# Seven-product gate and up in all four feed-forwards, with sums in place and SSM preparation moved to the down products

## The chip, the cores and the metric

The kernel runs on one core of one Trainium2 chip. The metric is the device time of one execution in microseconds (us). The engines are TensorE (PE, with its weight loads PEld), VectorE (DVE), ScalarE (ACT), GpSimd (POOL) and SyncE (SP), which issues most DMAs. Each engine works through its own instructions in order.

## The reference

One inference step of a trunk of two layers. Each layer adds half a feed-forward, a mixer, and half a second feed-forward to the residual x (1024 wide), all in fp32:

```python
def swiglu(h, w_gu, w_down):
    gate, up = jnp.split(h @ w_gu, 2, axis=-1)
    return (jax.nn.silu(gate) * up) @ w_down
...
every layer: x += 0.5*FFN_a(rms(x)); x += MIX(rms(x)); x += 0.5*FFN_b(rms(x))
```

In layer 0 the mixer is a depthwise convolution beside sliding-window attention, in layer 1 a grouped complex SSM with a GLU. There are 528 prompt positions (16 learned ones and 512 tokens) and 8 sample tokens, 536 columns in all. The hidden width of a feed-forward is 2816, which is 22 tiles of 128.

## The kernel before

x lies transposed in eight tiles x[0] to x[7] of 128 rows and 536 columns; a "half" is 268 of them. A product of fp32 precision is made of three matmuls of rounded parts: each operand is split into a part hi (written by ScalarE, L128, L226 or `put`'s L148) and the rest lo (subtracted on VectorE, L129, L227, L149), and TensorE adds hi·hi, hi·lo and lo·hi. Weights come by DMA into four buffers `raw`, and their parts go into three buffers `whi` and three `wlo`.

The four feed-forwards are called A, B (layer 0) and C, D (layer 1) here. `ffn` takes the 22 tiles in chunks of 8, 8 and 6: first gate and up of each tile of the chunk, which end in the subtraction that writes `ml`, then eight down products, each of which adds to one x tile (L428). After the last chunk `finalize` prepares the next stage's operands from x.

- In A and B a tile of gate and up is `gemm` twice: 96 matmuls of 268 columns. VectorE splits two weights (L129) and multiplies and adds (L406, L408, L409, L149).
- In C and D (`STRASSEN = (3, 5)`) `seven` makes a tile from seven products P1 to P7 of half the depth and half the columns, 84 matmuls (L268). It needs sums of weights (`seven_weights`, L230 to L235) and of operands (`operands`: xh, eh and fh with their lo parts), and additions afterwards (L272 to L290).

A tile framework orders the instructions of each engine from the code's priorities, its own time estimates and the buffers. Work that doesn't belong to a feed-forward is put between its steps by a generator, `filler`: `setup0` (tables for the first mixer) in A, and `ssm_prep` (tables for the SSM, mostly complex multiplications on VectorE at L877 to L883 and L1039 to L1046) in B, two steps after each gate and up tile but a chunk's last two, and two after each of six down products:

```python
                if filler is not None and i < nf - 2:
                    next(filler, None)
                    next(filler, None)
```

`load` brings in x, transposes it, and runs tile 0 of A's gate and up (`head`) product by product as each x tile arrives.

Of the kernel before, what the change touches and what calls it, by code (L numbers as in the profile page):

```python
# [18 lines left out]
D = 1024  # L19
# [13 lines left out]
STRASSEN, DMASUM = (3, 5), False  # L33
# [29 lines left out]
class Trunk:  # L63
# [87 lines left out]
    def finalize(self, d, g):  # L151

        nc = self.nc
        col = self.g[:, g * 8 + d:g * 8 + d + 1]
        x = self.x[d]
        if g in STRASSEN:
            self.operands(d, col)
# [17 lines left out]
    def extra(self, pool):  # L175

        self.fx = pool
# [29 lines left out]
    def seven_weights(self, gu, f):  # L207
# [1247 lines left out]
```

## Time and profile before

| | |
|---|---|
| Median of 3 runs | 2038.1 us (2034.99 to 2038.55) |
| Profiled execution | 2040.23 us |
| Its span in the trace | 2038.4 us |
| Busy: PE, DVE, ACT, POOL | 1978.1, 1378.6, 790.1, 113.5 us |
| Feed-forward A, from the load's end to the last x update | 48.7 to 428.7 us |
| First mixer | 428.7 to 662.9 us |
| Feed-forward B | 662.9 to 1068.0 us |
| Feed-forward C | 1068.0 to 1445.4 us |
| Second mixer and D | 1445.4 to 2038.4 us |

The span runs from the first to the last instruction that the profiler recorded; the execution's own time is 1.8 us longer. The stages are cut at the end of VectorE's update of x[7], since the next stage's first products need it soon after.

### The profile page before, as it was taken

The numbers are of one execution on the slowest core, as the hardware profiler recorded it, in microseconds if no ns is written. First come the engines' busy times: TensorE is split into PE (matmuls) and PEld (weight loads), VectorE is DVE, ScalarE is ACT, GpSimd is POOL, SyncE is SP. The second block draws the span as 40 slices with busy tenths as digits, with TensorE's granted clock in tenths as the row PEclk, the third lists the DMA queues.
The fourth block names the chain that finished last, engine by engine and source line by source line (L and its number), as shares of the span: only waits on it lengthen the run. The fifth ranks groups of instructions, "written<-read, shape, count | busy, mean of one in ns | idle before, by whom it ended". The sixth has DMA issues, their size and how long they took to land.

```text
span 2038.4 us, 37681 instructions
## 1 busy us (share of the span) xinstructions
PE 1978.1 (97%) x15774; PEld 1924.3 (94%) x15774; DVE 1378.6 (68%) x2263; ACT 790.1 (39%) x1274; POOL 113.5 (6%) x172
## 2 busy tenths in 40 slices
PE   6999999999989999999998999999999999999997
PEld 5999999998869999999998999999988999999997
DVE  4533433478977888666478859677795589587686
ACT  4322222333446332322255525345334455254353
POOL 2000000012200002112000000000110000000000
PEclk9999999999969999999999999999999999999998
DMA  6423333232005435446322323324783323233331
GB/s 177 123 87 90 89 88 94 73 85 59 27 6 122 124 127 161 127 122 172 103 83 78 109 83 94 104 83 148 191 260 109 89 73 111 87 94 94 94 92 55
DMA packets 371499, 213.52 MB, mean 105 GB/s; under 512 B 36119, under 2 KB 362323, under 8 KB 370921
## 3 DMA queue, kind: packets, MB, share of 16 engines
q1 hardware_dynamic: 354897, 190.63, 32.4%
q0 software_dynamic: 5872, 19.40, 3.3%
q8 instruction: 124, 2.03, 0.4%
q10 hardware_dynamic: 10560, 1.09, 0.4%
q14 instruction: 46, 0.38, 0.1%
HBM read 193.14 MB, written 23.65 MB: 106 GB/s over the span
## 4 chain that ended last, share of the span: by engine, by line
PE 89%; DVE 6%; ACT 2%; DMA 1%; issue 1%; SPq 1%; ACTq 0%; DVEq 0%
PE mm L139 28%; PE mm L268 19%; PE mm L142 14%; PE S L139 12%; PE S L142 6%; PE S L268 3%; DVE yc L566 1%; PE S L739 1%; DVE wlo L129 1%; DMA raw<-in_ffn_w_gu 1%; ACT whi L128 0%; PE ms L747 0%; PE ms L753 0%; DMA mC<-dC 0%; PE ms L1028 0%
## 5 line engine op out<-in xcount | busy, mean ns | idle before, releaser
L128 ACT ACTIVATE whi<-raw 128x1024 fp32r<-128x1024 f32 (+2 forms) x236 | 235.2, 1000 | 665.5 <-PE mm L139 314.5
L129 DVE TENSOR_TENSOR wlo<-raw,whi 128x1024 fp32r<-128x1024 f32 (+2 forms) x236 | 272.7, 1157 | 59.8 <-ACT whi L128 55.6
L139 PE MATMUL mm<-xh,whi 128*128 128x268 f32 x1280 | 268.5, 292 | 8.8 <-DVE us L1128 2.6
L139 PE MATMUL mm<-xl,whi 128*128 128x268 f32 x1280 | 266.7, 289 | 0.0
L142 PE MATMUL mm<-xh,wlo 128*128 128x268 f32 x1280 | 266.5, 289 | 0.0
L139 PE MATMUL mm<-mh,whi 128*128 128x268 f32 x1188 | 252.3, 290 | 2.5 <-DVE ta L286 1.2
L142 PE MATMUL mm<-mh,wlo 128*128 128x268 f32 x1188 | 249.9, 287 | 0.9 <-DVE wlo L129 0.8
L139 PE MATMUL mm<-ml,whi 128*128 128x268 f32 x1188 | 250.0, 287 | 0.0
L139 PEld LDWEIGHTS mm<-xh,whi 128*128 128x128 f32 x1280 | 201.8, 191 | 11.3 <-issue 3.6
L142 PEld LDWEIGHTS mm<-xh,wlo 128*128 128x128 f32 x1280 | 202.2, 190 | 2.0 <-issue 1.7
L139 PEld LDWEIGHTS mm<-xl,whi 128*128 128x128 f32 x1280 | 202.6, 191 | 1.1 <-issue 0.5
L139 PEld LDWEIGHTS mm<-mh,whi 128*128 128x128 f32 x1188 | 188.1, 189 | 4.9 <-ACT whi L128 1.8
L142 PEld LDWEIGHTS mm<-mh,wlo 128*128 128x128 f32 x1188 | 187.8, 188 | 2.0 <-DVE wlo L129 1.5
L139 PEld LDWEIGHTS mm<-ml,whi 128*128 128x128 f32 x1188 | 188.5, 189 | 0.2
L226 ACT ACTIVATE whi<-raw 128x1024 fp32r<-128x1024 f32 x88 | 93.4, 1061 | 104.1 <-issue 42.9
L139 PE MATMUL S<-mh,whi 128*128 128x268 f32 x604 | 128.4, 288 | 0.6 <-ACT whi L128 0.6
L139 PE MATMUL S<-ml,whi 128*128 128x268 f32 x604 | 127.3, 287 | 0.0
L142 PE MATMUL S<-mh,wlo 128*128 128x268 f32 x604 | 127.2, 286 | 0.0
L227 DVE TENSOR_TENSOR wlo<-raw,whi 128x1024 fp32r<-128x1024 f32 x88 | 107.4, 1221 | 15.8 <-ACT whi L226 14.9
L268 PE MATMUL mm<-xh,whi 128*128 128x268 f32 x352 | 103.2, 293 | 4.7 <-ACT sn L278 2.9
L268 PE MATMUL mm<-eh,whi 128*128 128x268 f32 x352 | 103.1, 293 | 0.9 <-issue 0.7
L268 PE MATMUL mm<-xl,whi 128*128 128x268 f32 x352 | 102.1, 290 | 0.0
(522 smaller groups left out, 4365.7 us busy)
## 6 DMA issues: line engine op xcount, KB each, us to landing
raw<-in_ffn_w_gu SPq DMA_DIRECT2D x174, 512.0 KB
raw<-in_ffn_w_down SPq DMA_DIRECT2D x64, 512.0 KB
raw<-in_ffn_w_down SPq DMA_DIRECT2D x32, 384.0 KB
raw<-in_ssm_w_glu SPq DMA_DIRECT2D x16, 512.0 KB
raw<-in_ab_w_in SPq DMA_DIRECT2D x10, 512.0 KB
dB<-B POOLq DMA_DIRECT2D x8, 512.0 KB, 3.8
dC<-CL POOLq DMA_DIRECT2D x32, 128.0 KB, 3.1
dT<-dK POOLq DMA_DIRECT2D x8, 512.0 KB, 5.0
```

What stands on the lines that cost most here:

```text
L128: nc.scalar.activation(hi[:, :K], raw[:, :K], AF.Copy)
L129: nc.vector.tensor_sub(lo[:, :K], raw[:, :K], hi[:, :K].bitcast(F32))
L139: nc.tensor.matmul(ps[:, h, :HT], hi[:, k, :], src[:, h * HT:(h + 1) * HT], start=(k == 0 and i == 0), stop=False)
L142: nc.tensor.matmul(ps[:, h, :HT], lo[:, k, :], xh[k][:, h * HT:(h + 1) * HT], start=False, stop=(k == K - 1))
L226: nc.scalar.activation(h[:], r[:], AF.Copy)
L227: nc.vector.tensor_sub(l[:], r[:], h[:].bitcast(F32))
L268: nc.tensor.matmul(ps, w[:, c + k, :], b[k], start=bool(first and k + i == 0), stop=bool(last and k == 3 and i == 2), skip_group_check=True)
L566: nc.vector.scalar_tensor_tensor(y, z, wcol(c, j), y, op0=OP.mult, op1=OP.add)
L739: nc.tensor.matmul(S[:, g, :w], qT[t][rw, 128 * b:128 * b + 128], kT[rw, k0:k0 + w], start=False, stop=True)
```

## The change

- `STRASSEN` holds all four feed-forwards, so A (but for tile 0, which stays in the load) and B use `seven` too.
- The chunks are 6, 8 and 8 tiles.
- The sums of weights are made in the `raw` buffers themselves; the buffer S goes.
- `operands` scales x anew (`scaled`) instead of keeping the scaled tiles of the first four.
- At the start of a feed-forward P1 and P5 of tiles 0 and 1 come first.
- The load makes `operands` too; for d below 4 it also splits the unsummed right half, into mh[4+d].
- `filler` runs over down products only: one step for each in a chunk of 6, two in a chunk of 8, one for four of the last chunk. `ssm_prep` therefore runs over B and C, and makes its table E in two halves.

```diff
-STRASSEN, DMASUM = (3, 5), False
+STRASSEN = (0, 2, 3, 5)
+CHUNKS = ((0, 6), (6, 8), (14, 8))
...
+    def scaled(self, d):
+        w = self.fx.tile([128, NT], F32, name="ou", bufs=2)
+        self.nc.scalar.activation(w[:], self.x[d][:], AF.Copy, scale=self.col(d))
+        return w
...
+        u = self.scaled(d)
         if d < 4:
...
-            self.put(self.xh[d][:], self.xl[d][:], w[:])
+            if plain:
+                self.put(plain[0][:, l], plain[1][:, l], u[:, r])
+            nc.vector.tensor_sub(u[:, r], u[:, l], u[:, r])
+            self.put(self.xh[d][:], self.xl[d][:], u[:])
             return
-        w, b = self.t1[k], self.b12[k]
-        u, e, f = t("ou"), t("oe"), self.fx.tile([128, HT], F32, name="of")
-        nc.scalar.activation(u[:], x[:], AF.Copy, scale=col)
         self.put(self.xh[d][:], self.xl[d][:], u[:])
-        nc.vector.scalar_tensor_tensor(e[:, l], w[:, r], -1.0, u[:, r], op0=OP.mult, op1=OP.subtract)
-        nc.vector.tensor_sub(e[:, r], u[:, r], b[:])
+        w = self.scaled(k)
+        e, f = self.fx.tile([128, NT], F32, name="sn", bufs=2), self.fx.tile([128, HT], F32, name="u3")
+        nc.vector.tensor_sub(e[:, r], u[:, r], w[:, r])
+        nc.vector.scalar_tensor_tensor(e[:, l], e[:, r], -1.0, w[:, l], op0=OP.mult, op1=OP.subtract)
         self.put(self.eh[k][:], self.el[k][:], e[:])
         nc.vector.scalar_tensor_tensor(f[:], e[:, l], -1.0, u[:, l], op0=OP.mult, op1=OP.subtract)
         self.put(self.fh[k][:], self.fl[k][:], f[:])
...
         split(gh, gl, G)
-        if not DMASUM:
-            nc.vector.tensor_add(S[:, k1], U[:, k0], U[:, k1])
-        nc.vector.tensor_add(S[:, k0], S[:, k1], G[:, k0])
-        split(sh, sl, S)
-        nc.vector.tensor_add(q[:], S[:, k0], G[:, k1])
-        if not DMASUM:
-            nc.vector.tensor_add(U[:, k0], U[:, k0], G[:, k0])
+        nc.vector.tensor_add(q[:], U[:, k0], U[:, k1])
+        split(qh, ql, q)
+        nc.vector.tensor_add(U[:, k0], U[:, k0], G[:, k0])
+        nc.vector.tensor_add(G[:, k0], G[:, k0], q[:])
+        nc.vector.tensor_add(G[:, k1], G[:, k1], G[:, k0])
+        split(sh, sl, G)
         split(uh, ul, U)
-        split(qh, ql, q)
...
+        early = {(0, "P1"): -4, (0, "P5"): -3, (1, "P1"): -2, (1, "P5"): -1} if f0 + n0 == 0 else {}
+        key = lambda a: early.get(a, 7 * a[0] + SLOTS[a[1]])
+        for n, p in sorted(((n, p) for n in range(nf - n0) for p in SLOTS), key=key):
...
             def products(k):
+                h, l = [self.xh[k][:, :HT], self.xh[k][:, HT:]], [self.xl[k][:, :HT], self.xl[k][:, HT:]]
+                if k < 4:
+                    h[1], l[1] = self.mh[4 + k][:, :HT], self.ml[4 + k][:, :HT]
                 for f in range(2):
-                    self.gemm(acc[f], (whi[f], wlo[f]), self.xh, self.xl, ks=(k,))
+                    for i, (w, b) in enumerate(((whi[f], h), (whi[f], l), (wlo[f], h))):
+                        for j in range(2):
+                            nc.tensor.matmul(acc[f][:, j, :HT], w[:, k, :], b[j], start=k + i == 0, stop=k + i == ND + 1)
...
-                nc.scalar.activation(self.xh[d][:], x, AF.Copy, scale=col)
-                nc.vector.scalar_tensor_tensor(self.xl[d][:], x, col, self.xh[d][:].bitcast(F32),
-                                               op0=OP.mult, op1=OP.subtract)
+                self.operands(d, (self.mh[4 + d], self.ml[4 + d]) if d < 4 else None)
...
-        for f0, nf in ((0, 8), (8, 8), (16, 6)):
-            if seven:
-                self.seven(gu, f0, nf)
-            for i in range(0 if seven else nf):
...
+        filler = iter(filler)
+        for f0, nf in CHUNKS:
+            last = f0 + nf == D_FF // 128
+            if f0 == 0 and head:
+                self.rstd()
...
-                self.put(self.mh[i][:], self.ml[i][:], b[:])
-                if filler is not None and i < nf - 2:
-                    next(filler, None)
-                    next(filler, None)
+                self.put(self.mh[0][:], self.ml[0][:], b[:])
+            self.seven(gu, f0, int(f0 == 0 and head is not None), nf)
...
-                if f0 == 16:
+                if last:
                     self.finalize(d, gnext)
-                if filler is not None and d < 6 and f0 < 16:
-                    next(filler, None)
-                    next(filler, None)
+                fill((1 if nf < 8 else 2) if not last else int(d < 4))
...
+        with self.tc.tile_pool(name="spe", bufs=1) as se:
+
+            for q0 in (0, 16):
+                qs = slice(q0, q0 + 16)
+                e = [se.tile([128, 16, NCK], F32, name=f"E{i}") for i in range(2)]
+                nc.vector.memset(e[0][:, :, 0], 1.0)
+                nc.vector.memset(e[1][:, :, 0], 0.0)
...
+                        if n > 4:
+                            yield
...
+                ZC = lambda: sj.tile([128, 1152], F32, name="Z")[:]
...
+                CL = ZC().rearrange("p (q r s c) -> p q r s c", q=4, r=2, s=9)
...
+        scope = self.extra()
+        self.project(2)
+        sp, fx = ExitStack(), []
         prep = self.ssm_prep(sp.enter_context(tc.tile_pool(name="sp", bufs=1)))
-
-        def then():
-            self.finish(prep)
-            sp.close()
-            self.extra(fx.enter_context(tc.tile_pool(name="fx", bufs=1)))
-
-        self.ffn(io["ffn2_w_gu"][0], io["ffn2_w_down"][0], 3, prep, then=then)
-        self.ffn(io["ffn1_w_gu"][1], io["ffn1_w_down"][1], 4, seven=fx)
-        fx = ExitStack()
-        self.mixer1(5, lambda: self.extra(fx.enter_context(tc.tile_pool(name="fx", bufs=1))))
-        self.ffn(io["ffn2_w_gu"][1], io["ffn2_w_down"][1], None, fin=True, seven=fx)
+        more = lambda: fx.append(self.extra())
+        self.ffn(io["ffn2_w_gu"][0], io["ffn2_w_down"][0], 3, scope, prep, then=more)
+        self.ffn(io["ffn1_w_gu"][1], io["ffn1_w_down"][1], 4, fx.pop(), prep)
+        self.finish(prep)
+        sp.close()
+        self.mixer1(5, more)
+        self.ffn(io["ffn2_w_gu"][1], io["ffn2_w_down"][1], None, fx.pop(), fin=True)
```

VectorE, among the down products of B's second chunk, before (x_80 is x[3], L1039 to L1046 and L878 to L883 are `ssm_prep`, w and Z its buffers):

```order
L428 SCALAR_TENSOR_TENSOR x_80<-S,x_80 128x536
L1041 TENSOR_TENSOR CL<-w_9945,w_9946 128x4x144
L129 TENSOR_TENSOR wlo<-raw,whi 128x1024
L1056 COPY BD<-bb 64x8x16 x2
L1065 TENSOR_TENSOR K<-ms,dd 128x16
L1043 TENSOR_TENSOR w_9945<-C,pw 128x576
L1044 TENSOR_TENSOR w_9946<-C,pw 128x576
L1045 TENSOR_TENSOR w_9945<-w_9945,w_9946 128x576
L1046 TENSOR_SCALAR CL<-w_9945 128x4x144
L878 TENSOR_TENSOR w_10265<-bb,pw 128x512
L877 TENSOR_TENSOR w_10264<-bb,pw 128x512
L428 SCALAR_TENSOR_TENSOR x_81<-mm,x_81 128x536
```

and after (`ssm_prep` at L877 and L1044 ff., x update L423, weights of the next gate and up at L222 to L229, down weights L130):

```order
L423 SCALAR_TENSOR_TENSOR x_80<-mm,x_80 128x536
L1044 TENSOR_TENSOR w_11246<-C,pw 128x576
L1045 TENSOR_TENSOR w_11247<-C,pw 128x576
L225 TENSOR_TENSOR q_10136<-raw 128x512
L130 TENSOR_TENSOR wlo<-raw,whi 128x1024
L227 TENSOR_TENSOR raw<-raw 128x512
L222 TENSOR_TENSOR ql<-q_10136,qh 128x512
L423 SCALAR_TENSOR_TENSOR x_81<-mm,x_81 128x536
L130 TENSOR_TENSOR wlo<-raw,whi 128x1024
L423 SCALAR_TENSOR_TENSOR x_82<-S,x_82 128x536
```

What moved: between these two x updates stood ten instructions of `ssm_prep` and one weight split; now two of `ssm_prep` stand between x[3] and x[4], with sums and splits of the next chunk's weights.

VectorE, among the gate and up tiles of B's second chunk, before (L406, L408, L409 and L149 are one tile's gate and up, L129 a weight split):

```order
L406 TENSOR_TENSOR ta<-S,R 128x536
L1046 TENSOR_SCALAR CL<-w_9317 128x4x144
L878 TENSOR_TENSOR w_9699<-bb,pw 128x512
L129 TENSOR_TENSOR wlo<-raw,whi 128x1024
L877 TENSOR_TENSOR w_9698<-bb,pw 128x512
L408 TENSOR_TENSOR tb<-mm,R 128x536
L409 TENSOR_TENSOR tb<-tb,ta 128x536
L879 TENSOR_TENSOR Z<-w_9698,w_9699 128x4x128
L129 TENSOR_TENSOR wlo<-raw,whi 128x1024
L881 TENSOR_TENSOR w_9698<-bb,pw 128x512
L882 TENSOR_TENSOR w_9699<-bb,pw 128x512
L149 TENSOR_TENSOR ml_114<-tb,mh_106 128x536
```

and after (L222 are splits, L225 and L227 to L229 sums of weights, L277, L283, L285 the additions and scalings of a tile):

```order
L222 TENSOR_TENSOR ql<-q_9303,qh 128x512
L228 TENSOR_TENSOR raw<-raw,q_9303 128x512
L277 TENSOR_TENSOR tb<-u_9195,mm 128x268
L285 TENSOR_TENSOR ta<-ta,R 128x536
L1050 TENSOR_TENSOR w_9804<-w_9804,w_9805 128x576
L229 TENSOR_TENSOR raw<-raw 128x512
L286 SCALAR_TENSOR_TENSOR tb<-tb,ta 128x536
L1051 TENSOR_SCALAR Z<-w_9804 128x4x144
L877 TENSOR_TENSOR w_9894<-bb,pw 128x512
L272 TENSOR_TENSOR ta<-sn,S 128x268
L876 TENSOR_TENSOR w_9893<-bb,pw 128x512
L222 TENSOR_TENSOR wlo<-raw,whi 128x1024
```

What moved: the tile's own rows come from `seven` and are more than twice as many, and rows of `ssm_prep`, issued at down products in the code, stand here still.

ScalarE at the start, before (L365 writes xh, L371 splits the head's weights, L374 makes squares, L362 copies x out of PSUM):

```order
L371 ACTIVATE whi<-raw 128x512
L362 ACTIVATE x_78<-S 128x536
L371 ACTIVATE whi<-raw 128x512
L365 ACTIVATE xh_86<-x_78,gcols 128x536
L374 ACTIVATE ta<-x_78 128x536
L365 ACTIVATE xh_85<-x_77,gcols 128x536
L374 ACTIVATE sq<-x_77 128x536
L362 ACTIVATE x_80<-S 128x536
L371 ACTIVATE whi<-raw 128x512
```

and after (L187 scales x into `ou`, L149 is `put`'s hi part, L373 and L376 what L371 and L374 were):

```order
L373 ACTIVATE whi<-raw 128x512
L366 ACTIVATE x_78<-S 128x536
L373 ACTIVATE whi<-raw 128x512
L376 ACTIVATE ta<-x_78 128x536
L187 ACTIVATE ou<-x_77,gcols 128x536
L376 ACTIVATE sq<-x_77 128x536
L187 ACTIVATE ou<-x_78,gcols 128x536
L366 ACTIVATE x_80<-S 128x536
L149 ACTIVATE mh_105<-ou 128x268
L149 ACTIVATE mh_106<-ou 128x268
L373 ACTIVATE whi<-raw 128x512
L376 ACTIVATE ta<-x_79 128x536
```

What moved: the two xh rows came right after the second weight split; now squares, scaled copies and hi parts of the right halves stand ahead of xh, which comes later than the rows shown.

## Rows read from the trace of the kernel before

**Rows 1.** The page: span, then busy time, share and instructions of each engine.
```profile
span 2038.4 us, 37681 instructions
...
PE 1978.1 (97%) x15774; PEld 1924.3 (94%) x15774; DVE 1378.6 (68%) x2263; ACT 790.1 (39%) x1274; POOL 113.5 (6%) x172
```

**Rows 2.** The page: shares of the chain that ended last, by engine.
```profile
PE 89%; DVE 6%; ACT 2%; DMA 1%; issue 1%; SPq 1%; ACTq 0%; DVEq 0%
```

**Rows 3.** Stretches: window, length, busy of PE, PEld, DVE, ACT, POOL, clock, DMA share, GB/s.
```profile
179.30:321.90 142.60, 142.60 (x1155) 142.60 (x1154) 56.69 (x65) 35.10 (x41) 0.00 (x0) 1.00 0.31 89
...
662.90:808.00 145.10, 145.10 (x1192) 143.76 (x1191) 126.15 (x323) 44.15 (x58) 14.33 (x27) 1.00 0.46 139
...
1068.00:1211.60 143.60, 136.76 (x1056) 134.02 (x1056) 108.59 (x162) 66.27 (x101) 0.00 (x0) 0.98 0.30 89
1211.60:1344.70 133.10, 132.42 (x1059) 131.10 (x1058) 97.74 (x137) 58.47 (x89) 0.00 (x0) 1.00 0.33 96
1344.70:1445.40 100.70, 99.58 (x794) 98.32 (x793) 78.03 (x110) 52.28 (x82) 1.35 (x5) 1.00 0.48 142
```

**Rows 4.** Busy time in pieces of these stretches, same columns.
```profile
1068.00:1155.30 87.30, 80.74 (x606) 78.21 (x606) 78.22 (x124) 51.18 (x83) 0.00 (x0) 0.96 0.29 85
1211.60:1309.50 97.90, 97.42 (x781) 96.62 (x780) 78.30 (x113) 49.77 (x80) 0.00 (x0) 1.00 0.33 98
1309.50:1344.70 35.20, 35.01 (x280) 34.48 (x279) 19.44 (x24) 8.69 (x9) 0.00 (x0) 1.00 0.31 91
1420.10:1445.40 25.30, 25.26 (x203) 24.87 (x201) 20.77 (x28) 15.48 (x22) 0.00 (x0) 1.00 0.86 253
200.00:260.00 60.00, 60.00 (x488) 60.00 (x487) 25.69 (x30) 16.56 (x20) 0.00 (x0) 1.00 0.31 91
...
1066.00:1090.00 24.00, 17.95 (x107) 16.04 (x106) 20.23 (x40) 13.11 (x22) 0.00 (x0) 0.86 0.15 44
```

**Rows 5.** Chain of waits, 1116 to 1147 us: start, length, engine, line, count.
```profile
1129.50 9.03 PE mm L268 x72
1138.54 1.49 PE S L268 x12
```

**Rows 6.** VectorE's instructions 663 to 1068 us by form: count, busy us, mean ns, idle before.
```profile
L129 DVE TENSOR_TENSOR wlo<-raw,whi 128x1024 fp32r<-128x1024 f32 x58 | 70.7, 1219 | 4.3 <-ACT whi L128 3.6
...
L149 DVE TENSOR_TENSOR ml<-tb,mh 128x536 fp32r<-128x536 f32 x22 | 15.6, 709 | 1.4 <-ACT mh L148 1.4
...
L1039 DVE TENSOR_TENSOR w<-C,pw 128x576 f32<-128x576 f32 x8 | 6.0, 754 | 0.2
```

**Rows 7.** VectorE, 1218 to 1224 us: start, length, line, operation.
```profile
1218.65 1.22 DVE L227 TENSOR_TENSOR wlo<-sraw,whi 128x1024 fp32r<-128x1024 f32 x1 [2.54 <-ACT whi L226]
1219.79 0.43 DVE L281 TENSOR_TENSOR tb<-u,mm 128x268 f32<-128x268 f32 x1
1220.13 0.68 DVE L230 TENSOR_TENSOR sraw<-raw 128x512 f32<-128x512 f32 x1
1220.85 0.69 DVE L231 TENSOR_TENSOR sraw<-sraw,raw 128x512 f32<-128x512 f32 x1
1221.46 0.68 DVE L235 TENSOR_TENSOR raw<-raw 128x512 f32<-128x512 f32 x1
```

**Rows 8.** ScalarE during the load: start, length, line, operation, idle before.
```profile
26.59 0.63 ACT L371 ACTIVATE whi<-raw 128x512 fp32r<-128x512 f32 x1 [6.19 <-DMA raw<-in_ffn_w_gu]
27.13 1.36 ACT L365 ACTIVATE xh<-x,gcols 128x536 fp32r<-128x536 f32 x2
...
37.95 0.62 ACT L362 ACTIVATE x<-S 128x536 f32<-128x536 f32 x1 [0.67 <-PE S L357]
38.60 0.74 ACT L365 ACTIVATE xh<-x,gcols 128x536 fp32r<-128x536 f32 x1
```

**Rows 9.** TensorE at the end of the load stage, same columns.
```profile
49.30 0.41 PE L142 MATMUL S<-xh,wlo 128*128 128x268 f32 x2
51.39 0.49 PE L139 MATMUL mm<-xh,whi 128*128 128x268 f32 x2 [1.68 <-DVE ta L406]
```

More of the change, by code (lines that the diff above doesn't have):

```diff
@@ L153, in finalize @@
         nc = self.nc
-        col = self.g[:, g * 8 + d:g * 8 + d + 1]
-        x = self.x[d]
+        self.col = lambda d: self.g[:, g * 8 + d:g * 8 + d + 1]
+        col, x = self.col(d), self.x[d]
         if g in STRASSEN:
-            self.operands(d, col)
+            self.operands(d)
         elif g < 6:
@@ L167, in finalize, with extra @@
             nc.vector.tensor_add(self.sq[:], self.sq[:], s[:])
-    def extra(self, pool):
-        self.fx = pool
+    def extra(self):
+        scope = ExitStack()
+        pool = self.fx = scope.enter_context(self.tc.tile_pool(name="fx", bufs=1, side="right"))
         t = lambda n, w: pool.tile([128, w], F32R, name=n)
@@ L290, in seven @@
                 nc.vector.scalar_tensor_tensor(b[:], b[:], -1.0, a[:], op0=OP.mult, op1=OP.mult)
-                self.put(self.mh[n][:], self.ml[n][:], b[:])
+                self.put(self.mh[n0 + n][:], self.ml[n0 + n][:], b[:])
                 del st[n]
@@ L381, in load, with ffn @@
         return acc
-    def ffn(self, wgu, wdn, gnext, filler=None, fin=None, head=None, seven=None, then=None):
+    def ffn(self, wgu, wdn, gnext, scope, filler=(), fin=None, head=None, then=None):
         nc, tc = self.nc, self.tc
@@ L389, in ffn, with fill @@
         R = halves(self.R[:])
-        for f0, nf in ((0, 8), (8, 8), (16, 6)):
-            if seven:
-                self.seven(gu, f0, nf)
-            for i in range(0 if seven else nf):
-                f = (f0 + i) * 128
-                if f or not head:
-                    pg = self.acc()
-                    self.gemm(pg, self.weights(gu[:, :, f:f + 128]), self.xh, self.xl)
-                if not f:
-                    self.rstd()
-                if f or not head:
-                    pu = self.acc()
-                    self.gemm(pu, self.weights(gu[:, :, D_FF + f:D_FF + f + 128]), self.xh, self.xl)
-                else:
-                    pg, pu = head
+        def fill(n):
+            for _ in range(n):
+                next(filler, None)
+        filler = iter(filler)
[3 more added lines that the diff above has]
+                self.rstd()
+                pg, pu = head
                 a, b = self.work("ta"), self.work("tb")
@@ L521, in setup0, with mixer0, _mixer0 @@
                        sk=sk, sk4=sk4, sks=sks, o512=o512, cw=cw, zs=zs, sc=sc, kcT=kcT, vc=vc)
-    def mixer0(self, p, gnext):
+    def mixer0(self, stage, gnext):
+        with self.tc.tile_pool(name="m0", bufs=1) as p:
+            self._mixer0(p, stage)
+    def _mixer0(self, p, stage):
         nc, io, out, ident = self.nc, self.io, self.out, self.ident
@@ L682, in samples @@
             nc.tensor.transpose(ps[:, :64], P[:64, 0, :128], ident[:64, :64])
-            pT = tl([128, 4, 128], "pT", bufs=3)
+            pT = stage.tile([128, 4, 128], F32, name="pT", bufs=3)
             nc.scalar.activation(pT[:, 0, :64], ps[:, :64], AF.Copy)
@@ L716, in last16 @@
                 nc.tensor.transpose(pt[:16, 256 + g * 128:384 + g * 128], P[:, g, 128:144], ident[:])
-            pT = tl([128, 4, 128], "pT", bufs=3)
+            pT = stage.tile([128, 4, 128], F32, name="pT", bufs=3)
             pa = pt[:].rearrange("p (a q) -> p a q", a=4)
@@ L742, in attend @@
                 pt = self.bank()
-                pTt = tl([128, 4, 128], "pT", bufs=3)
+                pTt = stage.tile([128, 4, 128], F32, name="pT", bufs=3)
                 n = len(kbs)
@@ L1023, in ssm_prep @@
                 yield
-                B = sj.tile([128, 1024], F32, name="B")
                 for i in range(2):
+                    B = sj.tile([128, 512], F32, name="B")
                     ps = self.bank()
```

138 lines of the change are left out of this document (60 added, 78 removed).

## The prediction

> **What bounds the kernel now.** I read the page first. TensorE is busy 97% of the span and VectorE 68% [rows 1], and TensorE has 89% of the chain that ended last, VectorE 6% [rows 2]. So matmuls that fall away shorten the kernel wherever VectorE can still feed TensorE, and the question is where it can't. The shares are means, so the view by stretches decides. A's second chunk of eight plain tiles and eight down products takes 142.60 us with TensorE busy throughout and VectorE for 56.69; B's first chunk, where `ssm_prep` runs, has VectorE at 126.15 of 145.10 us, and TensorE still full; C's second chunk, seven products and no preparation, takes 133.10 us with VectorE at 97.74 [rows 3]. In its gate and up alone, VectorE is busy 78.30 of 97.90 us; the other 35.20 us belong to the down products, with VectorE at 19.44 [rows 4]. Seven-product tiles beside preparation stand nowhere in this trace.
>
> **TensorE's part.** A plain tile has 96 matmuls; in a steady stretch 488 take 60.00 us [rows 4], 0.123 each, so a tile takes 11.9 with the pace of whole chunks (142.60 us less 8 x 48 x 0.124 of down products, over 8). A seven-product tile has 84 at 9.03/72 = 0.1254 us [rows 5], 10.5 us. That is 1.36 us less for a tile. 43 tiles change (A's 21, B's 22): 516 matmuls and 59 us if nothing else counts (not 516 x 0.123 = 63, since the matmuls of a seven-product tile follow each other a little more slowly). But a whole chunk of eight only falls from 142.60 to 133.10 [rows 3], 9.5 us, since each chunk loses about 1.3 us where it begins and ends; by that measure 43 tiles are worth 51 us. I take the pace of 10.5 with these 1.3 us added.
>
> The Trainium skill, "TensorE: Matmul & The Clock Gate", section "Back-to-back issue gap", gives an isolated matmul at full clock as N/2.4 + 2.5 ns, 114 ns at 268 columns, and warns that a stream of weight loads and matmuls is set by both. The trace has 125 ns. By the page's figure the 516 matmuls would be an estimated 58.9 us instead of the 63 at the row's pace.
>
> **VectorE's part.** Its busy time counts overlapping ends once, so I price rows start to start: the 128x1024 split lasts 1.22 us but the next row starts 1.14 later; 512-wide sums start 0.61 to 0.72 apart though they last 0.68, a 268-wide one 0.34 [rows 7]. The same 0.08 taken off 0.709 gives 0.63 for 536 columns, and off 0.754 gives 0.67 for the 576-wide multiplications of the preparation [rows 6]. Counting rows in the order of the changed kernel from the last x update to the last `ml` of B's second chunk: 22 splits 25.1, 33 sums and short splits (0.60) 19.8, 24 half-width additions 8.2, 24 full ones 15.1, eight `ml` 5.0, three down splits 3.4, together 76.6 us (78.30 was measured for the same work in C [rows 4]); and on top 113 rows of `ssm_prep`, 31.9 us. The code issues them at the down products, but there VectorE holds sums and splits of the next chunk, as the order's pieces show, and the preparation runs on into gate and up. The total is 108.5 us, above the 97.90 that TensorE needs there. The same count for the others: B's first chunk 72.2 + 17.6 = 89.8, C's first 63 + 27.0 = 90.0; a six-tile gate and up took 87.30 us from the start of C, of which 8 to 9 were lost to operands and clock [rows 4], so TensorE needs about 80 to 85. B's third (85.1) and C's second and third (79.7, 76.6) stay below 97.90. So three stretches, 288.3 us together, become VectorE's.
>
> What does VectorE reach when it is the bound? It works in order and waits for ScalarE's hi parts and TensorE's products. Upper bound: 100%. Lower: the start of C, where it is busy 20.23 of 24.00 us, 84%, in rows that depend on one another [rows 4]. Nearer to what comes is B's first chunk with 87% while TensorE was the bound and VectorE had room to wait [rows 3]; nothing shows a stretch it bounds for long. Weights are split one tile ahead (three buffers for three splits), so most waits are covered; I take 97%.
>
> **The sum**, against the span of 2038.4 us:
> - A. The load is longer. xh of the last x tile now comes directly behind the copy, at 38.60 [rows 8]; the head's last matmul starts at 49.30 and the next tile at 51.39 [rows 9]. In the changed order the first xh stands behind some six more ScalarE rows (0.6 to 0.7 each, from 26.59), and for d of 4 and above there is a serial chain through both engines (scaled copy, hi part, subtraction, another, hi part) of about 4 us each with two `ou` buffers. I put the last xh at 54 and the first seven-product matmul at 58.4, 7 us later than now. From there five tiles at 10.5, down products of six tiles 35.7, twice (84.3 + 47.6) and 4 us at chunk ends make 356: A ends at 414.4, 14 earlier. Bounds: no delay in the load (-21) and 15 us of it (-6).
> - First mixer and projection: pools opened and closed in another order, +2 (0 to +4).
> - B: 89.8/0.97 + 26 for the six-tile down products (25.30 was measured in C's chunk of six, from its last `ml` to its last x update [rows 4]) + 108.5/0.97 + 35.20 + 133.10 = 399, before 405.1: -6.
> - C: 90.0/0.97 + 26 + 133.10 + 133.10 = 385; before 143.60 + 133.10 + 100.70 = 377.4 [rows 3]: +7.5. What B loses in preparation, C takes up.
> - Second mixer and D: P1 and P5 of tiles 0 and 1 need only the first four operands, so the start is covered better, and the last chunk has eight tiles rather than six; -3 (-6 to 0).
>
> Sums in place, rescaling and the shared buffer are in the row counts. They cost order, not rows: a sum that overwrites `raw` waits for ScalarE's split of the same buffer, covered by the tile of lookahead; uncovered it is one ScalarE split, about 1 us, for each tile. Together: -14 + 2 - 6 + 7.5 - 3 = -13.5, a span of 2025 and an execution of about 2026.7. The profiled one stood 2.1 above the median, so against the median the forecast is **2025 us**.
>
> **The rivals.**
> - *Preparation hidden.* VectorE's surplus goes into the down products, where it was busy 19.44 of 35.20 us [rows 4]; then B is 85 + 25.3 + 35.2 + 98 + 133.1 = 376.5 (-29) and C the same (-1), and the sum is -14 + 2 - 29 - 1 - 3 = -45: 1993 us. For it: TensorE was full in B's first chunk beside 87% [rows 3]. Against: the pieces of the order, which put the preparation in gate and up.
> - *VectorE waits (slower).* The rows of both kinds of work share an in-order queue: a `ssm_prep` row that writes the shared buffer Z waits for TensorE's transposes of its last content, behind which splits and products' additions wait, and TensorE then waits for those splits. At the 84% of C's start [rows 4] the three stretches take 343 us rather than 297, +46: 2071 us. It decides below 92.8%: there the 288.3 us cost 13.5 more than at 97%, and the gain is gone. Operand chains where a stage starts showed 84%; steady tiles with lookahead should do better.
> - *The pipeline empties.* A next row that never starts before the last has ended would cost 0.08 us for each of the 628 VectorE rows in the three stretches: +50, 2075 us. [Rows 7] show 1219.79 inside a row that lasts to 1219.87, so I give it 0.03. This is the Trainium skill, "VectorE: DVE Perf Modes", section "The DRAIN you can't avoid": the next operation does not start until the pipe is empty. By that rule the change is slower; the starts in this trace disagree.
> - *No change.* The load longer by 15 us and VectorE at 95%: +8 and +6 on the forecast, 2039 us; or the losses at the starts of stages stay (C's 143.60 against 133.10 [rows 3]).
>
> **How the numbers follow.** Forecast and its neighbourhood (VectorE at 94 to 100%, 2012 to 2036): 0.45. Hidden: 0.13. VectorE waiting: 0.26, the emptied pipeline 0.03, no change 0.13. Measurements tell from no change what is over 0.2%, 4 us. Faster takes 0.40 of the forecast and the hidden 0.13: 0.53. The same takes 0.05 of the forecast's edge and 0.11 of no change: 0.16. Slower has the waiting, the emptied pipeline and 0.02 of no change: 0.31. The range reaches from near the hidden case to a VectorE at 87%, 1998 to 2060; about one in ten is left out on either side. Its own range for the forecast is 2012 to 2036.
>
> **What would show it.** In the profile after: TensorE's matmuls fall by some 500 and its busy time by some 60 us; VectorE's busy time rises by about 250 us. A's second chunk is near 133 us at a full TensorE. In the gate and up of B's second chunk TensorE has idle time that ends on VectorE's splits, the stretch takes about 112 us, and VectorE is over 95% busy; if it is under 93% there, with its own waits on ScalarE or TensorE, the slower rival is right; if it takes 98, the hidden one. C is longer than before. The load's last head matmul is near 57. The forecast is wrong if the order of VectorE's queue makes TensorE wait in stretches that I count as TensorE's (C's second and third chunk, A), or if the half clock that C's start has (0.86 over 24 us [rows 4]) comes at every chunk that waits.

## The result and the profile after

The changed kernel takes 2094.54 us (median of four runs, 2094.25 to 2096.19), the kernel before 2036.55 us (four runs too): a ratio of 1.0288, 95% interval 1.0273 to 1.0303. It is 58 us slower; the forecast was 2025 us, with a range that ends at 2060.

The page of the profiled execution after has this span, busy time and chain, to be read beside [rows 1, 2]:

```profile
span 2093.0 us, 37652 instructions
...
PE 1947.2 (93%) x15242; PEld 1867.4 (89%) x15242; DVE 1622.2 (78%) x2768; ACT 951.5 (45%) x1577; POOL 120.5 (6%) x183
...
PE 65%; DVE 19%; issue 6%; ACT 6%; DMA 3%; ACTq 0%; SPq 0%; POOL 0%; DVEq 0%; POOLq 0%
```

TensorE has 532 matmuls fewer, yet only 30.9 us less busy time, and its share of the chain that ended last has gone from 89% to 65%; what it lost there VectorE, ScalarE and issue have. So the removed work is real, and TensorE waits for more than it saved. Where it waits, the stretches tell (columns as in [rows 3]): first whole stages (B, C, and the second mixer with D), then chunks of eight tiles (A's second, C's third, D's second):

```profile
671.10:1089.20 418.10, 386.25 (x2989) 371.68 (x2990) 368.99 (x766) 201.50 (x313) 20.67 (x38) 0.98 0.36 105
1089.20:1490.20 401.00, 379.36 (x3027) 367.65 (x3026) 318.30 (x472) 183.94 (x284) 28.42 (x53) 1.00 0.41 121
1490.20:2093.00 602.80, 568.70 (x4719) 556.74 (x4718) 429.08 (x716) 256.77 (x404) 17.17 (x34) 0.99 0.37 107
```

```profile
158.10:297.20 139.10, 133.32 (x1058) 131.00 (x1057) 98.42 (x136) 59.59 (x89) 0.00 (x0) 1.00 0.33 92
...
1351.00:1490.20 139.20, 133.47 (x1059) 131.15 (x1058) 102.46 (x143) 67.30 (x102) 1.36 (x5) 1.00 0.44 127
1798.50:1938.80 140.30, 133.74 (x1058) 131.13 (x1058) 98.54 (x137) 59.59 (x89) 0.00 (x0) 1.00 0.32 92
```

Read the second fence first. These chunks hold no preparation, VectorE is busy 98 to 102 us, and TensorE runs as many matmuls, at a full clock, as in C's second chunk before; but they take 139 to 140 us where that one took 133.10, with VectorE at 97.74 [rows 3]. D, whose products are the same in number as before, lost as much a chunk as A, which is new to `seven`. Six chunks can be set against those 133.10 us: A's second and third, B's third, C's second and third, D's second. They took 139.1 to 141.6, which makes 43 of the 68 us between the span that was forecast (2025) and the one measured (2093.0). (B's third and C's second hold some preparation too.)

What the loop waits for shows in the chain of waits of C's third chunk, 1351 to 1408 us (start, length, engine, line, count; steps are left out at the dots):

```profile
1374.54 0.38 ACT tb L280
...
1384.62 0.68 DVE raw L227
1385.30 1.15 DVE wlo L222
1386.49 2.97 PE mm L264 x22
...
1395.32 0.61 ACT whi L221
...
1396.29 0.62 ACT mh L149
...
1397.78 0.38 ACT tb L280
1398.20 3.29 PE mm L264 x24
```

TensorE waits twice in each pair of tiles: at 1386.49 P6 waits for a lo split that VectorE ended just before, and at 1398.20 P3 waits for the copy of P4 (L280) out of the PSUM tile into which P3 adds too; the copy stands on ScalarE behind hi splits. The same copy comes at 1374.54 and 1397.78: 23.24 us for 168 matmuls that need 21.1 at the pace of [rows 5], 2.2 us lost in two tiles. Over a whole chunk the two waits come to 5.8 us, here in A's second (us in total, times, longest):

```profile
PE mm L264 <- ACT tb L280: 3.3, 3, 1.1
PE mm L264 <- DVE wlo L222: 2.5, 4, 0.6
```

In C's second chunk before, TensorE waits 0.7 us in all, and for neither of the two:

```profile
PE mm L268 <- ACT sn L278: 0.5, 1, 0.5
PE mm L139 <- ACT whi L128: 0.2, 1, 0.2
```

When the split at 1385.30 could start, ScalarE's own rows of the same place tell:

```profile
1384.12 1.06 ACT L221 ACTIVATE whi<-raw 128x1024 fp32r<-128x1024 f32 x1 [0.76 <-PE S L264]
1385.56 1.06 ACT L221 ACTIVATE whi<-raw 128x1024 fp32r<-128x1024 f32 x1 [0.38 <-PE mm L264]
```

Both hi splits wait for TensorE, the first for a product that ends in the PSUM tile S (P2), the second for one in mm. A split reads only `raw`, so what it can await from TensorE is its place in the ring (the three buffers of `whi`, and as many of `wlo`, are the ring's places), which a product still reads. The lo splits at 1385.30 and after come behind them. But the kernel before has the same two waits in its own loop, for the PSUM tiles S and mm (L226 is its split):

```profile
1253.57 1.06 ACT L226 ACTIVATE whi<-raw 128x1024 fp32r<-128x1024 f32 x1 [0.28 <-PE S L268]
1255.00 1.06 ACT L226 ACTIVATE whi<-raw 128x1024 fp32r<-128x1024 f32 x1 [0.37 <-PE mm L268]
```

So such waits on ScalarE show that the ring had no place to spare for these splits in either kernel; what made it worse, only the experiments can tell.

### The profile page after: what moved, and what is told of

It is laid out like the page before. It is cut to its first block, busy times and chain, and to the rows that moved or that the text cites. A ratio compares the mean times of both kernels' runs of the same rounds, so it can differ in the third digit from the quotient of the medians.

```text
span 2093.0 us, 37652 instructions
## 1 busy us (share of the span) xinstructions
PE 1947.2 (93%) x15242; PEld 1867.4 (89%) x15242; DVE 1622.2 (78%) x2768; ACT 951.5 (45%) x1577; POOL 120.5 (6%) x183
## 4 chain that ended last, share of the span: by engine, by line
PE 65%; DVE 19%; issue 6%; ACT 6%; DMA 3%; ACTq 0%; SPq 0%; POOL 0%; DVEq 0%; POOLq 0%
PE mm L264 24%; PE mm L140 16%; PE mm L143 8%; PE S L140 7%; DVE wlo L222 4%; PE S L143 3%; PE S L264 3%; ACT whi L221 2%; DMA raw<-in_ffn_w_gu 2%; DVE yc L563 1%; DVE ql L222 1%; DVE raw L228 1%; DVE ta L285 1%; DVE raw L229 1%; DVE ta L283 1%
## 5 line engine op out<-in xcount | busy, mean ns | idle before, releaser
L221 ACT ACTIVATE whi<-raw 128x1024 fp32r<-128x1024 f32 x261 | 274.4, 1058 | 258.5 <-PE mm L264 93.2
L222 DVE TENSOR_TENSOR wlo<-raw,whi 128x1024 fp32r<-128x1024 f32 x261 | 317.9, 1219 | 23.2 <-ACT whi L221 23.1
L129 ACT ACTIVATE whi<-raw 128x1024 fp32r<-128x1024 f32 (+2 forms) x150 | 143.4, 966 | 308.3 <-PE mm L140 160.2
L264 PE MATMUL mm<-xh,whi 128*128 128x268 f32 x696 | 206.0, 296 | 40.8 <-ACT tb L280 35.9
L264 PE MATMUL mm<-eh,wlo 128*128 128x268 f32 x696 | 204.0, 293 | 27.1 <-DVE wlo L222 27.1
L130 DVE TENSOR_TENSOR wlo<-raw,whi 128x1024 fp32r<-128x1024 f32 (+2 forms) x150 | 167.1, 1120 | 61.2 <-ACT whi L129 59.7
L264 PE MATMUL mm<-el,whi 128*128 128x268 f32 x696 | 199.2, 286 | 0.0
L264 PE MATMUL mm<-xl,whi 128*128 128x268 f32 x696 | 198.9, 286 | 0.0
L264 PEld LDWEIGHTS mm<-eh,wlo 128*128 128x128 f32 x696 | 131.4, 189 | 36.0 <-DVE wlo L222 36.0
L264 PEld LDWEIGHTS mm<-eh,whi 128*128 128x128 f32 x696 | 131.3, 189 | 1.8 <-ACT whi L221 1.7
L264 PEld LDWEIGHTS mm<-el,whi 128*128 128x128 f32 x696 | 131.5, 189 | 0.0
```

The lines of the kernel that those rows point to most:

```text
L129: nc.scalar.activation(hi[:, :K], raw[:, :K], AF.Copy)
L130: nc.vector.tensor_sub(lo[:, :K], raw[:, :K], hi[:, :K].bitcast(F32))
L221: nc.scalar.activation(h[:], r[:], AF.Copy)
L222: nc.vector.tensor_sub(l[:], r[:], h[:].bitcast(F32))
L264: nc.tensor.matmul(ps, w[:, c + k, :], b[k], start=bool(first and k + i == 0), stop=bool(last and k == 3 and i == 2), skip_group_check=True)
```

## The experiments

**Which part of the new weight preparation.** Two things were changed at once in the weights: sums are made in place, and P5 now reads the short sum q while P3, the last product of a tile (slot 11 of `SLOTS`; P5 has slot 5), reads the second half of S. The second of them, an exchange of roles, stands neither in the list under "The change" nor in the lines of the diff shown there. Four kernels tell the two apart. `b_` is the kernel before with an edit in C and D alone, `a_` the changed kernel with an edit; line numbers in what follows are each kernel's own.

`b_swap`, roles exchanged, S in its own buffer:

```diff
...
+        nc.vector.tensor_add(q[:], U[:, k0], U[:, k1])
+        split(qh, ql, q)
+        nc.vector.tensor_add(U[:, k0], U[:, k0], G[:, k0])
+        nc.vector.tensor_add(S[:, k0], G[:, k0], q[:])
+        nc.vector.tensor_add(S[:, k1], G[:, k1], S[:, k0])
         split(sh, sl, S)
...
-                "P3": (qh, ql, 0, X(self.xh[4:], r), X(self.xl[4:], r)),
+                "P3": (sh, sl, 4, X(self.xh[4:], r), X(self.xl[4:], r)),
...
-                "P5": (sh, sl, 4, X(self.xh[:4], r), X(self.xl[:4], r)),
+                "P5": (qh, ql, 0, X(self.xh[:4], r), X(self.xl[:4], r)),
```

> The kernel before, with only the roles of two weight sums exchanged in C and D (P5 from the short sum q = U0+U1, P3 from the second half of S), S still in a buffer of its own. Theory 1, held buffer: P3 is the last product of a tile, so S's hi and lo buffers come free 6 slots later, the ring of three turns too late, and an eight-tile chunk of C or D takes about 140 us rather than 133.1 (TensorE waits for wlo and for the copy of P4). Four such chunks and two of six tiles: about +35 us, 2072. Theory 2, sums in place: nothing is in place here, so 133 us a chunk and 2037.

`b_inplace`, sums in place, roles as before:

```diff
         split(gh, gl, G)
...
+        nc.vector.tensor_add(q[:], U[:, k0], U[:, k1])
+        nc.vector.tensor_add(U[:, k0], U[:, k0], G[:, k0])
+        nc.vector.tensor_add(G[:, k0], G[:, k0], q[:])
+        split(sh[:, k0], sl[:, k0], G[:, k0])
+        split(sh[:, k1], sl[:, k1], q)
+        nc.vector.tensor_add(G[:, k1], G[:, k1], G[:, k0])
         split(uh, ul, U)
...
+        split(qh, ql, G[:, k1])
```

> The kernel before, with the sums of C and D made in place in raw and q but with the products' roles as before (P5 from the S buffer's second half, P3 from the short sum); S is split in two pieces, one more ScalarE and one more VectorE row a tile, 0.1 to 0.2 us each. Theory 1, held buffer: 133 us a chunk, total within 0.3% of 2037. Theory 2, sums in place: the chain of G split, sums in G, S split makes the weights late, 139 to 140 us a chunk, total about 2072.

`b_both`, the new `seven_weights` whole:

> The kernel before with the whole new weight preparation in C and D (in place and roles exchanged), nothing else. Both theories: 139 to 141 us for an eight-tile chunk, total about 2072. If it stays at 133 us and 2037, the loss comes from another part of the change (first products, rescaled operands, shared sn and u3 buffers).

`a_old`, the changed kernel with the body of `b_inplace`:

> The changed kernel with the products' roles as before, sums in place as in the change (S split in two pieces). Theory 1: the seven eight-tile chunks fall from 139 to 141 us to about 133, with what the chunks of six gain in all 50 to 55 us, total about 2042. Theory 2: unchanged, 2094.

Measured, beside 2037.13 us for the kernel before on the same chip:

| kernel | median us | ratio, 95% |
|---|---|---|
| `b_swap` | 2070.60 | 1.0160 (1.0143 to 1.0177) |
| `b_inplace` | 2034.28 | 0.9989 (0.9977 to 1.0000) |
| `b_both` | 2066.96 | 1.0141 (1.0124 to 1.0158) |
| `a_old` | 2042.74 | 1.0025 (1.0013 to 1.0038) |

C's second chunk in `b_swap`, `b_both` and `b_inplace`, each by its own windows:

```profile
1215.50:1354.60 139.10, 133.45 (x1058) 131.15 (x1057) 98.97 (x136) 60.40 (x89) 0.00 (x0) 1.00 0.31 92
```

```profile
1213.50:1352.80 139.30, 133.47 (x1059) 131.18 (x1058) 98.46 (x137) 59.59 (x89) 0.00 (x0) 1.00 0.31 91
```

```profile
1205.80:1339.20 133.40, 132.31 (x1058) 130.87 (x1057) 98.59 (x144) 59.54 (x97) 0.00 (x0) 1.00 0.32 96
```

The exchanged roles cost 6 us a chunk by themselves, the sums in place nothing; and undone in the changed kernel they give back 51.8 us of its 58. What is left, a ratio of 1.0025, is still no gain.

**Is it the buffer, or the order of the sums?** `b_own` is `b_both` with two buffers of its own for S's hi and two for its lo, so that the ring serves G and U alone:

```diff
-        sh, sl = (self.wts.tile([128, 8, 128], F32R, name=n, bufs=3) for n in ("whi", "wlo"))
+        sh, sl = (self.fx.tile([128, 8, 128], F32R, name=n, bufs=2) for n in ("shi", "slo"))
...
```

> The kernel before with the whole new weight preparation of C and D (which alone took 2067), but S's hi and lo parts in two buffers each of their own instead of a third place in the ring (and one scratch tile shared to make room). Held buffer: with two buffers, S of the next tile no longer waits for P3 of this one; eight-tile chunks fall back to 133 to 134 us and the total to 2034 to 2040. Rival, the order of the new preparation itself (short sum first, S last) makes weights late: 139 to 140 us a chunk, 2067.

```profile
1203.60:1337.70 134.10, 132.91 (x1059) 131.10 (x1058) 97.77 (x137) 58.36 (x89) 0.00 (x0) 1.00 0.32 95
```

With the roles exchanged and the sums in the same order as in `b_both`, but the buffers no longer shared, the chunk is back at 134.10 from 139.30, and TensorE's waits in it at 1.1 us from 5.9. So it is the buffer. The total, 2043.64 us, ratio 1.0040 (1.0027 to 1.0052), is 4 to 10 us above what was expected; its ten runs spread from 2033.89 to 2045.58 and the profiled one, 2033.89, is the lowest, so its trace does not show where the others' time went. That stays open.

**What the preparation costs beside seven products.** `a_late` is `a_old` with no filler in B and C; the preparation stands alone behind C.

```diff
-        self.ffn(io["ffn2_w_gu"][0], io["ffn2_w_down"][0], 3, scope, prep, then=more)
-        self.ffn(io["ffn1_w_gu"][1], io["ffn1_w_down"][1], 4, fx.pop(), prep)
+        self.ffn(io["ffn2_w_gu"][0], io["ffn2_w_down"][0], 3, scope, then=more)
+        self.ffn(io["ffn1_w_gu"][1], io["ffn1_w_down"][1], 4, fx.pop())
```

> The changed kernel with the old roles (2042.7), but no step of the SSM preparation inside B and C; all of it stands behind C. What counts is the length of B and C, not the total. VectorE bound by the preparation: B falls from 408 to about 382 (starts lost as now) and C from 391 to about 378, so the preparation costs about 40 us inside seven-product feed-forwards. Rival, the preparation is hidden and B and C are long for their starts: both within 5 us of now. Total about 2043 - 40 + 110 to 140 us for the preparation alone, some 2110 to 2145.

Its total is 2155.22 us (ratio 1.0585, 1.0569 to 1.0601), more than expected by 10: alone, the preparation costs 150. B's and C's lengths are what it was made for. `a_old` first: B, C; B's first gate and up, its second, and C's first; then `a_late`, the same stretches:

```profile
652.70:1060.70 408.00, 384.10 (x2992) 373.08 (x2993) 369.19 (x789) 203.53 (x335) 20.60 (x38) 0.97 0.36 108
1060.70:1452.10 391.40, 380.14 (x3023) 371.09 (x3023) 319.36 (x495) 186.02 (x305) 28.11 (x53) 0.99 0.42 124
...
652.70:747.90 95.20, 83.40 (x600) 79.48 (x601) 91.49 (x257) 55.26 (x96) 0.00 (x0) 0.89 0.25 74
775.10:879.10 104.00, 96.72 (x755) 93.91 (x754) 97.53 (x217) 51.20 (x85) 4.16 (x8) 1.00 0.42 128
...
1060.70:1157.60 96.90, 88.17 (x683) 83.01 (x686) 93.18 (x163) 49.76 (x87) 18.99 (x35) 0.95 0.44 128
```

```profile
657.50:1044.90 387.40, 371.56 (x2914) 364.91 (x2914) 302.42 (x467) 195.36 (x319) 0.00 (x0) 0.98 0.32 92
1044.90:1419.70 374.80, 366.64 (x2907) 361.16 (x2908) 296.25 (x529) 182.89 (x298) 0.00 (x0) 1.00 0.33 96
...
657.50:750.90 93.40, 79.80 (x588) 76.46 (x589) 74.92 (x127) 52.02 (x89) 0.00 (x0) 0.91 0.26 75
776.20:872.00 95.80, 94.67 (x755) 93.43 (x754) 80.23 (x122) 50.76 (x87) 0.00 (x0) 1.00 0.35 100
...
1044.90:1127.50 82.60, 76.64 (x594) 74.23 (x595) 77.27 (x211) 47.87 (x83) 0.00 (x0) 1.00 0.27 79
```

The preparation costs 20.6 us in B and 16.6 in C. With it VectorE is busy 94 to 96% of the three stretches, without it 80 to 94%, and C's first falls by 14.3, B's second by 8.2. (The framework has put some 100 of the small rows of the preparation into C's start in `a_late` too, so C's 16.6 is the least that it costs.) B's first falls by 1.8 only, though VectorE then has 18 us to spare: that stretch is long for its start.

Not all of this is VectorE's. The preparation has rows on TensorE too, transposes (L1034) and products (L1066), all of them in B and C in `a_old` and behind C in `a_late` (`a_old`: count, busy us, mean ns, idle before):

```profile
L1034 PE MATMUL ms<-ident,Z 128*128 128x128 f32 x64 | 9.8, 276 | 0.0
L1066 PE MATMUL ms<-Z,BD 128*32 128x128 f32 x128 | 7.0, 284 | 1.6 <-ACT ta L285 1.0 <-DVE Z L1047 0.6
```

They keep TensorE busy for 16.8 us, nearly half of the 37.2. In B's second stretch the matmuls are equal in number (755), so its 8.2 us are not theirs; C's first has 89 matmuls more in `a_old`, and TensorE's busy time alone accounts for 11.5 of its 14.3 us.

**The early products.** `a_noearly` is `a_old` with P1 and P5 of the first tiles in their usual places:

```diff
-        early = {(0, "P1"): -4, (0, "P5"): -3, (1, "P1"): -2, (1, "P5"): -1} if f0 + n0 == 0 else {}
+        early = {(0, "P1"): -4, (0, "P5"): -3, (1, "P1"): -2, (1, "P5"): -1} if False else {}
```

> The changed kernel with the old roles (2042.7), without the order that puts P1 and P5 of tiles 0 and 1 first. If that order is what shortens the start of D (585 us from C's end against 593 before) and of B and C: +2 to +3 us for each of four feed-forwards, about 2052. If not: 2043, and D's gain is the chunks of 6, 8, 8.

2056.22 us, ratio 1.0106 (1.0080 to 1.0131). B, C, and the second mixer with D:

```profile
651.50:1067.00 415.50, 386.95 (x2993) 373.94 (x2993) 369.89 (x789) 202.75 (x335) 20.11 (x38) 0.97 0.36 106
1067.00:1466.20 399.20, 381.65 (x3023) 371.37 (x3022) 319.60 (x494) 186.43 (x305) 28.08 (x53) 0.99 0.42 122
1466.20:2051.80 585.60, 563.84 (x4720) 554.93 (x4718) 429.70 (x739) 257.52 (x426) 17.51 (x34) 0.99 0.38 110
```

B and C take 7.5 and 7.8 us more, D nothing (585.60 against 585.10 in `a_old`). The order is worth more than expected, but only in B and C (A never had it: there tile 0 stays in the load, `f0 + n0` is 1 and `early` is empty); D's gain of 8 us over before comes from something else, the chunks' lengths or the rest of the new code.

**Preparation beside plain tiles.** `hyb` has A, C and D as in `a_old`; B is plain, in chunks of 8, 8 and 6, with all the preparation over it as before the change:

```diff
-STRASSEN = (0, 2, 3, 5)
+STRASSEN = (0, 3, 5)
...
+        def then():
+            self.finish(prep)
+            sp.close()
+            more()
+        self.ffn(io["ffn2_w_gu"][0], io["ffn2_w_down"][0], 3, None, prep, then=then, plain=True)
```

> Seven products in A, C and D with the old roles, sums in place and early products; B plain in chunks of 8, 8 and 6 with all the preparation over its gate, up and down products, as before the change. If the preparation does not fit beside seven products (VectorE) but fits beside plain ones: B 405 and C 375 to 380, the total 2043 - 3 - 13 = about 2027. If A's gain of 9 us is lost elsewhere or the start of C stays long: 2034 to 2040.

2031.66 us, ratio 0.9973 (0.9960 to 0.9986): the lowest median of all. C took 379.30 us, B 409.40 rather than 405, with TensorE busy for 408.66 of them:

```profile
657.30:1066.70 409.40, 408.66 (x3375) 403.66 (x3373) 289.24 (x615) 131.44 (x178) 47.31 (x86) 1.00 0.42 126
```

**The preparation on GpSimd.** `a_pool` is `a_old` with GpSimd instead of VectorE for the multiplications, sums and negation of Z and CL, 104 rows in all; the first of those lines:

```diff
-                nc.vector.tensor_mul(v(w[0]), cr, pr)
+                nc.gpsimd.tensor_mul(v(w[0]), cr, pr)
...
```

> The changed kernel with the old roles (2042.7), with the large multiplications of the preparation (12 rows of 512 or 576 columns for each of eight groups, and one negation) on GpSimd instead of VectorE: about 65 us of VectorE rows fall away in B and C. GpSimd's multiplications of 536 columns in the first mixer took 1.88 us, so these 104 rows take about 200 us there, within the 800 us of B and C. VectorE bound: B and C, 408.0 and 391.4 us, come down by about half of the 37 us that the preparation was seen to cost, total 2015 to 2027. Rival, GpSimd and VectorE hinder each other, or the preparation's chain gets so long that TensorE's rows of it come late: no gain, 2040 or more.

2094.09 us, ratio 1.0282 (1.0264 to 1.0299): 51 slower than `a_old`. GpSimd and VectorE around 1121 to 1126 us:

```profile
1119.53 2.11 POOL L882 TENSOR_TENSOR w<-bb,pw 128x512 f32<-128x512 f32 x1
...
1123.05 1.36 POOL L883 TENSOR_TENSOR Z<-w,w 128x512 f32<-128x512 f32 x1
1124.49 1.51 POOL L1045 TENSOR_TENSOR w<-C,pw 128x576 f32<-128x576 f32 x1
```

```profile
1120.94 0.42 DVE L283 TENSOR_TENSOR ta<-sn,mm 128x268 f32<-128x268 f32 x1
...
1122.74 2.24 DVE L226 TENSOR_TENSOR raw<-raw 128x512 f32<-128x512 f32 x1
1124.90 1.68 DVE L284 TENSOR_TENSOR ta<-ta,R 128x536 f32<-128x536 f32 x1
```

A 512-wide sum, 0.68 us in [rows 7], lasts 2.24 beside rows of GpSimd, while a row that reads PSUM keeps its 0.42 beside the multiplication that runs from 1119.53. Over B and C VectorE has 104 rows fewer than in `a_old` (1180, 1284) and yet is busy for 716.0 us instead of 688.6: what left it came back as longer rows. TensorE waits for it longer, 19.7 us for an addition of a tile (L278) and 11.7 for lo splits, in `a_old` 5.0 and 3.4; for GpSimd's Z it waits 1.2 us in all, so the late rows that the rival named as well do not show. The Trainium skill, "SBUF — State Buffer", section "SBUF: two separate sides", has a VectorE instruction with two SBUF inputs and a GpSimd one share a port pair that the first to start holds alone. That the rows get longer agrees; the order does not show it, since the sum starts at 1122.74, ahead of the multiplication at 1123.05, and is the one that gets longer.

**The preparation later.** `a_spread` is `a_old` with fewer filler steps in B and more in C, so that all eight groups of large multiplications stand in C:

```diff
-                fill((1 if nf < 8 else 2) if not last else int(d < 4))
+                fill(((1 if nf < 8 else 2) if not last else int(d < 4)) if head else int(not last) if even else 2)
```

> The changed kernel with the old roles (2042.7), its preparation issued later: one step for each down product of B's first two chunks, none in its last, and two for each down product of C, so that all eight groups of the large multiplications stand in C (four in its first, four in its second chunk). VectorE bound only where the preparation is dense: B falls from 408 to 392 to 398 us, C's first chunk stays near 122 and its second grows from 135 to about 140; total about 2032 to 2036. If what the preparation costs is the same wherever it stands: B and C together stay at 799 us, total 2043.

2059.37 us, ratio 1.0118 (1.0101 to 1.0135). B came down to 399.50 us, but C grew to 412.40, its second chunk to 152.20 where 140 was expected (135.1 in `a_old`, the second fence):

```profile
649.60:1049.10 399.50, 378.25 (x2933) 369.24 (x2934) 348.86 (x747) 200.05 (x328) 7.73 (x14) 0.97 0.34 100
1049.10:1461.50 412.40, 388.36 (x3082) 375.12 (x3081) 339.85 (x535) 189.55 (x312) 40.93 (x77) 0.98 0.44 128
1175.20:1327.40 152.20, 142.17 (x1138) 136.84 (x1138) 122.03 (x192) 64.30 (x107) 17.77 (x32) 0.99 0.42 122
```

```profile
1183.20:1318.30 135.10, 134.00 (x1083) 132.24 (x1082) 101.64 (x151) 60.96 (x100) 4.96 (x8) 1.00 0.36 107
```

Both theories failed: neither is the cost the same everywhere, nor did C's second chunk have room. VectorE is only 80% busy there, so a bound by its rows alone does not explain 152 us. TensorE has 55 matmuls more than in `a_old`, rows of the preparation, and is busy 8.2 us longer; what delays it for the other 9 us was not tested.

## Why the prediction was wrong

**The step that failed** is the one on buffers: "Weights are split one tile ahead (three buffers for three splits), so most waits are covered", and with it "Sums in place, rescaling and the shared buffer are in the row counts. They cost order, not rows". I counted splits per tile and did not ask which product reads each part last. Before, the three places of the ring came free after P2 (G), P5 (S) and P4 (U), in slots 1, 5 and 9; the short sum that P3 reads in slot 11 lay outside the ring. After, S is read until P3. Two places are then held almost to the tile's end, and the next tile's P6 and P7 in slots 10 and 13 must get their parts through these or through the one place that P2 frees. Which split takes which place the trace doesn't say. Hi and lo splits come just in time, and P4's copy queues behind them. `b_swap` shows that the exchange alone does it, `b_own` that it is the buffer. The forecast carried the 133.10 us of [rows 3], or the same sum, over to chunks which then took 139 to 142 us. With the roles put back in `a_old` they took 133.2 to 135.1; only B's third stayed at 141.2, for another reason (below). The forecast named the exchanged roles nowhere; they are two lines of the whole diff.

With the roles put back, the terms of the sum can be read one by one in the trace of `a_old` (an execution of 2039.11 us, 3.6 below the median):

| stage, us | before | forecast | after | `a_old` |
|---|---|---|---|---|
| end of A | 428.7 | 414.4 | 437.5 | 419.3 |
| first mixer | 234.2 | 236 | 233.6 | 233.4 |
| B | 405.1 | 399 | 418.1 | 408.0 |
| C | 377.4 | 385 | 401.0 | 391.4 |
| second mixer and D | 593.0 | 590 | 602.8 | 585.1 |

- **A and the load.** The first run of seven-product matmuls starts at 58.20 us in `a_old`, where I had 58.4; but after twelve of them TensorE waits for ScalarE's hi split, and the steady run starts at 62.95. TensorE's rows (start, length, line, idle before):

```profile
58.20 0.37 PE L265 MATMUL mm<-xh,whi 128*128 128x268 f32 x1
...
62.95 0.39 PE L265 MATMUL mm<-xh,whi 128*128 128x268 f32 x1 [3.02 <-ACT whi L221]
```

  From there A takes what was worked out. The direction was right, the size 4.5 us short.
- **VectorE as the bound.** The three stretches were to take 92.6, 111.9 and 92.8 us; `a_old` has 95.20, 104.00 and 96.90, VectorE at 94 to 96% instead of 97. Their sum, 296.1, is near the forecast's 297.2 by luck: the three missed by +2.6, -7.9 and +4.1 us. C's first has much of its length from TensorE's own rows of the preparation, as `a_late` shows, and for B's first the reason was another again: without the preparation it still takes 93.40 us. There the granted clock is 0.50, its half level of 1.2 GHz, from 657 to 675 us in `a_old`, with TensorE busy 11.82 of the 18 us and waiting mostly for operands in the rest; before the clock fell TensorE was busy for 0.48 of 4.30 us (652.70 to 657.00):

```profile
657.00:675.00 18.00, 11.82 (x44) 9.40 (x44) 17.82 (x74) 12.51 (x24) 0.00 (x0) 0.50 0.20 60
```

- **B and C besides.** What was missed is that the preparation costs in the other pieces too: B's third chunk took 141.2 us in `a_old`, not 133.1, and its second chunk's down products 40.4 instead of 35.2:

```profile
879.10:919.50 40.40, 40.40 (x348) 39.37 (x347) 33.30 (x54) 11.57 (x16) 10.87 (x20) 1.00 0.49 150
```

  TensorE is busy through all of these, with 348 matmuls where [rows 4] have 280. The sum priced the preparation on VectorE alone and put its rows on TensorE, 16.8 us in B and C, at nothing; B and C of `a_old` together are 15.4 us over their forecast. How much of that is these rows and how much are waits was not told apart.
- **Second mixer and D.** The gain was 7.9 us, not 3, and the first reason given for it, the early products, was worth nothing there (`a_noearly`).
- **The rivals.** The hidden preparation fell: `a_late` has B and C 37 us shorter. The waiting VectorE was not the cause of the 58 us: B's laden second chunk gave back 7 us in `a_old` (151.7 to 144.4), as much as chunks without preparation. The prediction's sign of being wrong did come, TensorE waiting in A and in C's second and third chunk, but through the ring and not through the order of VectorE's queue: `b_own` keeps the new order of sums and splits and loses the waits. The emptied pipeline would have made the three stretches 347 us; they took 296. The section of the Trainium skill that the prediction names there ("VectorE: DVE Perf Modes", "The DRAIN you can't avoid") itself says that a next operation which is not held starts earlier, so the starts in the trace do not contradict it.
- **No preparation in plain B.** `hyb` confirms what remains of the mechanism. Beside plain tiles TensorE is idle for 0.74 us of B's 409.40, so the preparation can cost there little more than its own rows on TensorE (15.0 us, and 14.0 in the kernel before), against 37 us beside seven products. The seven products of A gain 6 us there (422.9 at A's end) and 9 in `a_old`, net of a longer load.

In the changed kernel itself, B's first two gate and up stretches took 96.30 and 116.30 us: both effects together, not told apart there.

## What to carry to other kernels

When storage is exchanged between equal sums, list for each buffer of a ring the last reader before and after: a ring of three serves three splits a tile only while each place is given back in time for the split that takes it next. Carry a measured chunk time over to changed code only if its buffers' lifetimes are unchanged. And a filler that fits beside one form of a loop has to be priced anew beside a form that loads the same engine more, and on every engine on which it has rows; `hyb`, which keeps the two apart, is 0.3% under the kernel before.

## What had not been expected of the hardware

In `a_pool` multiplications on GpSimd, 1.2 to 1.4 us each in the mean for 512 or 576 columns, and the sums behind them lengthened VectorE's rows with two SBUF inputs: a 512-wide sum (L226) from 0.69 us in the mean to 0.87, one of them to 2.24. Rows with an input from PSUM kept their 0.43 us. Moving 104 rows off VectorE made the kernel 51 us slower.
